# A hybrid encoder block on one core: a fourth early pair of the up-projection, one behind each late token tile

## The chip, the cores and the metric

The kernel runs on one core of a Trainium2 chip. Its time is device time in microseconds of that core; each number below is the median of several executions, or comes from one profiled execution. TensorE multiplies matrices into PSUM (eight banks of 128 x 512 float32), VectorE and ScalarE do elementwise work and read PSUM, GpSimd does small things, and SyncE (SP) and ScalarE issue DMAs. Each engine works its instructions off in order and waits at the head of its queue for what the next one needs.

## What is computed

1024 tokens of width 1024 pass a mixing block (pooling and neighbourhood attention, joined by an output projection with a residual) and a squared-ReLU MLP with a hidden width of 4096, each behind an RMS norm:

```python
def reference(x, norm_mix_g, w_in, w_pool, pool_scale, rpb, w_out,
              norm_mlp_g, w_up, w_down, final_g):
    for l in range(DEPTH):
        h = rmsnorm(x, norm_mix_g[l])
        proj = h @ w_in[l]
        ...
        a = pool_mixer(u, w_pool[l], pool_scale[l])
        b = neighbourhood_attention(q, k, v, rpb[l])
        x = x + jnp.concatenate([a, b], axis=-1) @ w_out[l]
        h = rmsnorm(x, norm_mlp_g[l])
        x = x + jnp.square(jax.nn.relu(h @ w_up[l])) @ w_down[l]
    return rmsnorm(x, final_g)
```

All of it is float32, and DEPTH is 1.

## The kernel before

**Products.** A float32 operand is split into a high part (cast to float32r, on ScalarE) and a low part (what the cast left, on VectorE); each product of two 128-wide blocks is then three matmuls (`three`, lines 143, 145, 147): high by high, high by low, low by high. A *product* in the text below sums four such blocks: 12 matmuls of 128 x 512.

**The MLP's products** are done in Strassen-Winograd form: tokens and the contraction are halved, so that the 1024 x 1024 operand becomes seven operands of 512 x 512 (`ops[1]` to `ops[7]`, tiles `hop`), and `w_up` is taken in 16 *pairs* `b` of 2 x 128 columns, each giving seven products (b, 1) to (b, 7). Products 1 and 2 of a pair need plain parts of the operand (`ops[1]`, `ops[2]`, from the first four token tiles) and plain quarters of the weights; the others need sums. Product 1 goes to a bank `ps_x`, on which products 6 and 7 add later; 2 goes to `ps_e`, 5 and 3 to `ps_w`, 4 to `ps_z`.

**The passage.** After attention the kernel records an order by hand (`manual_schedule`), from one pool of eight PSUM banks (`psum2`, tiles `ps_...`). For each of eight token tiles `tt`:

- `out_tile(tt)`: 24 matmuls of the output projection into two banks (`ps_o`), two VectorE sums with the residual (`acc`), the sum of squares on ScalarE (line 118), `rs` on GpSimd, and `hn`, the normalized tile, on VectorE (line 843, put off into `rest`). SyncE stores the tile to `x2` (line 835) and loads the residual of tile `tt + 2`. Tiles 0 to 3 also prepare the attention's share for tiles 4 to 7: `msp`, a cast and a low part.
- `halfway(tt)`: eight transposes into two banks `ps_t`, then `operands`: copies, casts and low parts of `hop`. Tiles 4 to 7 also form the sums of the Winograd operands.

Between the late tiles stand three *early pairs*: `load_early` (SyncE loads 512 KB, `uraw`), `split_early` (casts and low parts, `us`), `early_pair` (products 1 and 2 of pair `b`, 24 matmuls), and `early_done` (a copy of `ps_x`, a sum with `ps_e`, ReLU and square, and a store of `r11` to DRAM by SyncE, line 870). `EARLY = 3` is their count.

**Low parts** are not recorded at once: `cut2` puts them into a list `lows`; `vec`, which records a VectorE sum, records one low part behind it, and `due(keys)` records all up to those named. What is in the list thus decides which low part VectorE does when.

**The late sequence.** `load_up(b)` loads weights (`wraw`, 1 MB, line 912) into three buffers; `cut(b, i)` forms and splits the weights of a product (`s`); `multiply` records a product; `evacuate` reads it out of its bank: copies (line 999), sums, ReLU and square (lines 855, 856), stores. `seq` is the order of the products: first 2, 3, 4, 5, 6, 7 of the early pairs without 1 and 2, then the seven of pairs 3 to 15. `queue` gives the cuts, five products ahead. `u2` is a pool of 15 buffers for the sums. At the head of this sequence `last_steps` finishes the operands of tile 7. The down-projection follows with the same kind of products (`ps_a`, `ps_b`).

Of the kernel before, what the change touches and what calls it, by code (L numbers as in the profile page):

```python
# [9 lines left out]
F32R = mybir.dt.float32r  # L10
AF = mybir.ActivationFunctionType
ALU = mybir.AluOpType
PSUM = bass.MemoryType.PSUM
# [16 lines left out]
KR = 12  # L30
NPAIR = 16
NARROW, WIDE = 13, 3
EARLY = 3
LOADS, CUTS, STAGGERED = 10, 4, 4


# [1 line left out]
def block_kernel(ctx, tc, x, norm_mix_g, w_in, w_pool, pool_scale, rpb, w_out,  # L38
# [13 lines left out]
    pad0.tile([P, 88], F32, name="padding0")  # L52
    const = ctx.enter_context(tc.tile_pool(name="const", bufs=1))
    dram = ctx.enter_context(tc.tile_pool(name="dram", bufs=1, space=DRAM))
    banks = [tc.tile_pool(name="psum", bufs=2, space=PSUM), tc.tile_pool(name="psum2", bufs=8, space=PSUM)]
    firstp = ExitStack()
    psum = [firstp.enter_context(banks[0])]
    small = ctx.enter_context(tc.tile_pool(name="small", bufs=4))
# [14 lines left out]
    def t4(name, dt=F32):  # L73
        return k4.tile([P, 1024], dt, tag="k4", name=name, bufs=NARROW)
# [632 lines left out]
    ops = {i: t_op(hb) for i in (1, 5, 2, 3, 4)}  # L707
    ops.update({i: t_op(ka) for i in (6, 7)})

    def load_early(b):  # L710
        raw = t4("uraw").rearrange("p (c n) -> p c n", c=NC8)
        nc.sync.dma_start(out=raw, in_=w_up[:, 2 * b * P:(2 * b + 1) * P]
                          .rearrange("(c p) n -> p c n", p=P))
        return raw

    firstp.close()
    psum[0] = ctx.enter_context(banks[1])
# [12 lines left out]
    def due(*keys):  # L730

        while any(k in keys for k, _ in lows):
            lows.pop(0)[1]()
# [6 lines left out]
    def cut2(key, hi, lo, src):  # L740
        nc.scalar.copy(out=hi, in_=src)  # L741
        low(key, lo, src, hi)

    def split_early(raw, b):
        out = []
        for k in range(2):
            s = t4("us", F32R).rearrange("p (l c n) -> p l c n", l=2, c=4)
            cut2(("us", b, k), s[:, 0], s[:, 1], raw[:, 4 * k:4 * k + 4, :])
            out.append(s)
        return out  # L750

    def product(ps, s, t, more=False):

# [19 lines left out]
    def turn(hn):  # L773
        pts = []
        for g in range(2):
            pt = bank("t")
            for k in range(4):
                c = 4 * g + k
                nc.tensor.transpose(pt[:, k * P:(k + 1) * P], hn[:, c * P:(c + 1) * P], ident)
            pts.append(pt.rearrange("p (k t) -> p k t", k=4))  # L780
        return pts
# [38 lines left out]
    nc.sync.dma_start(out=gb2, in_=norm_mlp_g[0].partition_broadcast(P))  # L820
    px, pe, pw, pz = {}, {}, {}, {}
    r11, r12, r21, r22 = {}, {}, {}, {}
    raw_early, early, hns, turned_ = {}, {}, {}, {}
    rest = []

    def out_tile(tt):
        while rest:
            rest.pop(0)()
        a = acc[tt]
        for nh in range(2):  # L830
            nsl = slice(nh * HALF, (nh + 1) * HALF)
            ps = bank("o")
            run(out_half(mb[tt // 4], wos[1], tt, nh, ps))
            vec(a[:, nsl], ps, a[:, nsl], ALU.add)
        nc.sync.dma_start(out=x2[tt * P:(tt + 1) * P, :], in_=a)
        load_acc(tt + 2)
        hns[tt] = t4("hn2")
        rs = rstd([sumsq(a, hns[tt])])
        if tt < 4:
            m = t4("msp", F32R).rearrange("p (l t) -> p l t", l=2)  # L840
            cut2(("mb1", tt), m[:, 0], m[:, 1], bs[tt][:, HALF:])
            mb[1].append(m)
        rest.append(lambda: nc.vector.scalar_tensor_tensor(out=hns[tt], in0=a, scalar=rs, in1=gb2,
                                                           op0=ALU.mult, op1=ALU.mult))

    def halfway(tt):

        steps = operands(turn(hns.pop(tt)), tt)
        steps[:] = steps[:2] + rest + steps[2:]
        rest.clear()  # L850
        for s in steps:
            s()
# [5 lines left out]
    def early_pair(b):  # L858
        due(("us", b, 0), ("us", b, 1), ("op", 1), ("op", 2))
        px[b], pe[b] = bank("x"), bank("e")  # L860
        product(px[b], early[b][0], ops[1])
        product(pe[b], early[b][1], ops[2])

    def early_done(b):
        t = t4("r11")
        r, m = t[:, :HALF], t[:, HALF:]
        nc.scalar.copy(out=m, in_=px[b])
        vec(r, pe[b], m, ALU.add)
        relu_square(r)
        nc.sync.dma_start(out=us[0][b], in_=r)  # L870

    for tt in range(4):
        out_tile(tt)
        if tt:
            halfway(tt - 1)
    raw_early[0] = load_early(0)
    due(*[("mb1", k) for k in range(4)])
    out_tile(4)
    halfway(3)
    raw_early[1] = load_early(1)  # L880
    early[0] = split_early(raw_early[0], 0)
    out_tile(5)
    halfway(4)
    early_pair(0)
    out_tile(6)
    early_done(0)
    raw_early[2] = load_early(2)
    early[1] = split_early(raw_early[1], 1)
    halfway(5)
    out_tile(7)  # L890
    halfway(6)
    early_pair(1)
    while rest:
        rest.pop(0)()
    early[2] = split_early(raw_early[2], 2)
    pts7 = turn(hns.pop(7))
    early_done(1)
    early_pair(2)
    last_steps = operands(pts7, 7)
    last_steps.pop(0)()  # L900
    early_done(2)
    first.close()


# [92 lines left out]
    def copied(ps, name):  # L997
        c = tu(name)
        nc.scalar.copy(out=c, in_=ps)
        return c  # L1000

    def evacuate(b, i):

        if i == 1:
            m1[b] = copied(px[b], "m1")
        elif i == 5:
            m5[b] = copied(pw[b], "m5")
        elif i == 6:
            m16[b] = copied(px[b], "m16")
        elif i == 2:  # L1010
            r11[b] = relu2(pe[b], m1[b])
            stored(1, b, r11[b])
        elif i == 7:
            m167[b] = copied(px[b], "m167")
            r22[b] = relu2(px[b], m5[b])
            stored(4, b, r22[b])
        elif i == 3:
            r12[b] = relu2(pw[b], m16[b])
            if b < EARLY:
                r11[b] = tu("r11")  # L1020
                nc.sync.dma_start(out=r11[b], in_=us[0][b])
        else:
            r21[b] = relu2(m167[b], pz[b], ALU.subtract)
            stored(2, b, r21[b])
            u_sums(b)
# [46 lines left out]
    def cut_pair(i, b):  # L1072
# [11 lines left out]
        if ahead:  # L1084
# [2 lines left out]


    seq = [(0, 5), (0, 6), (1, 5), (1, 6), (0, 7), (0, 3), (0, 4), (2, 5), (2, 6), (1, 7), (1, 3), (1, 4),
           (2, 7), (2, 3), (2, 4)]  # L1090
    seq += [(b, i) for b in range(EARLY, NPAIR) for i in (1, 5, 6, 2, 7, 3, 4)]
    queue = list(seq)
    for k in range(2):
        cut(*queue.pop(0))
        last_steps.pop(0)()
    cut(*queue.pop(0))
    last_steps.pop(0)()
    loads, splits = order_d[:LOADS], order_d[:CUTS]
    for n, x in enumerate(seq):
        while queue and seq.index(queue[0]) <= n + 5:  # L1100
            cut(*queue.pop(0))
        multiply(*x)
        if n >= 1:
            evacuate(*seq[n - 1])
        if lazy and x[1] != 7:
            lazy.pop(0)()
        left = len(seq) - 1 - n
        if left <= 5:
            for _ in range(2):
                if loads:  # L1110
                    load_d(*loads.pop(0))
        if left <= 2:
            cut_pair(*splits.pop(0))
# [154 lines left out]
```

## Time and profile before

| | us |
|---|---|
| median of three runs | 1029.84 (1028.5 to 1030.84) |
| the profiled execution | 1031.89 |
| its span, first to last instruction | 1030.1 |
| TensorE busy | 982.0 (95%) |
| VectorE busy | 662.3 (64%) |
| ScalarE busy | 537.7 (52%) |
| GpSimd busy | 174.8 (17%) |

The mean granted clock of TensorE is 0.981 of full speed. TensorE is nearly always busy, so a share of busy time says little here; what matters is where its 48 us of idle time and the stretches at a lower clock lie. The windows view gives busy time by engine for any stretch, with the granted clock; the timeline gives each instruction with the idle time before it and what ended that; the chain follows the work that ended last.

### The profile page before, as it was taken

To read this page: it belongs to the slowest core of one execution; us is meant where nothing else is said; L and a number is where in the kernel's file an instruction comes from. 1 tells how busy PE (TensorE), PEld (TensorE's weight loads), DVE (VectorE), ACT (ScalarE), POOL (GpSimd) and SP (SyncE) were. 2 spreads that over 40 slices of the span, in tenths; PEclk is the share of its full clock that TensorE was granted. 3 is DMA by queue.
4 is the path that set the end of the run, shared out by engine and by line. 5 is a ranking of instruction groups with operands and counts; after the bars stand their busy time and mean duration, and the time that the engine had idled before them with its cause. 6 is when DMAs were issued, how large, how long until landed. Compare 5 with 4: busy or idle time off the path is not lost.

```text
span 1030.1 us, 13174 instructions
## 1 busy us (share of the span) xinstructions
PE 982.0 (95%) x4508; PEld 811.8 (79%) x4508; DVE 662.3 (64%) x1165; ACT 537.7 (52%) x1045; POOL 174.8 (17%) x228
## 2 busy tenths in 40 slices
PE   7998999999899896599999999999999999999996
PEld 5786888887787774488888888888888888888885
DVE  6512588577665557577656656654677868649774
ACT  6413666567652545366556556555544544445463
POOL 3613436252530110000000000000020202003211
PEclk9999999999899997799999999999999999999998
DMA  8585333504761431465554554528966434355222
GB/s 290 153 236 129 76 94 82 145 23 106 247 209 75 174 132 62 133 214 175 159 171 130 158 168 123 164 82 286 341 221 229 160 104 162 103 203 186 86 102 100
DMA packets 103685, 159.40 MB, mean 155 GB/s; under 512 B 9409, under 2 KB 48833, under 8 KB 103618
## 3 DMA queue, kind: packets, MB, share of 16 engines
q1 hardware_dynamic: 103040, 157.51, 48.2%
q10 hardware_dynamic: 578, 1.05, 0.3%
q8 instruction: 35, 0.57, 0.2%
q14 instruction: 32, 0.26, 0.1%
HBM read 105.83 MB, written 48.27 MB: 150 GB/s over the span
## 4 chain that ended last, share of the span: by engine, by line
PE 83%; DMA 3%; issue 3%; DVE 3%; ACT 2%; POOL 2%; SPq 2%; ACTq 0%; POOLq 0%; DVEq 0%
PE ps_pp L143 5%; PE ps_pp L145 5%; PE ps_pp L147 5%; PE ps_a L145 5%; PE ps_a L143 5%; PE ps_a L147 5%; PE ps_x L147 4%; PE ps_b L145 4%; PE ps_b L143 4%; PE ps_b L147 4%; PE ps_x L143 4%; PE ps_x L145 4%; PE ps_w L143 3%; PE ps_w L145 3%; PE ps_w L147 3%
## 5 line engine op out<-in xcount | busy, mean ns | idle before, releaser
L100 ACT CAST st<-ur 128x512 fp32r<-128x512 f32 x112 | 69.7, 622 | 133.0 <-PE ps_a L147 61.4
L101 DVE TENSOR_TENSOR st<-ur,st 128x512 fp32r<-128x512 f32 x112 | 82.8, 739 | 80.8 <-ACT st L100 80.3
L1130 POOL TENSOR_TENSOR m<-m,x2t 128x512 f32<-128x512 f32 x16 | 27.3, 1729 | 519.0 <-DMA x2t<-x 402.3
L147 PE MATMUL ps_a<-st 128*128 128x512 f32 x256 | 99.7, 390 | 0.0
L143 PE MATMUL ps_a<-st 128*128 128x512 f32 x256 | 99.7, 389 | 0.0
L145 PE MATMUL ps_a<-st 128*128 128x512 f32 x256 | 99.7, 389 | 0.0
L101 DVE TENSOR_TENSOR st<-pq,st 128x512 fp32r<-128x512 f32 x112 | 84.5, 754 | 1.1
L143 PE MATMUL ps_pp<-hh,wh 128*128 128x512 f32 x192 | 76.7, 399 | 2.0 <-DVE q L468 2.0
L145 PE MATMUL ps_pp<-hl,wh 128*128 128x512 f32 x192 | 76.6, 399 | 0.0
L147 PE MATMUL ps_pp<-hh,wl 128*128 128x512 f32 x192 | 76.4, 398 | 0.0
L100 ACT CAST st<-pq 128x512 fp32r<-128x512 f32 x112 | 69.0, 616 | 13.6 <-DVE pq L1077 13.5
L143 PE MATMUL ps_b<-st 128*128 128x512 f32 x192 | 74.8, 390 | 0.0
L145 PE MATMUL ps_b<-st 128*128 128x512 f32 x192 | 74.8, 389 | 0.0
L147 PE MATMUL ps_b<-st 128*128 128x512 f32 x192 | 74.8, 389 | 0.0
L855 ACT ACTIVATE r<-r 128x512 f32<-128x512 f32 x64 | 40.5, 632 | 65.0 <-DVE r L736 65.0
L143 PE MATMUL ps_x<-hop,s 128*128 128x512 f32 x180 | 70.2, 390 | 0.0
L145 PE MATMUL ps_x<-hop,s 128*128 128x512 f32 x180 | 70.1, 390 | 0.0
L147 PE MATMUL ps_x<-hop,s 128*128 128x512 f32 x180 | 70.1, 389 | 0.0
L528 POOL TENSOR_SCALAR s<-s,ri 128x288 f32<-128x288 f32 (+1 forms) x64 | 42.5, 667 | 109.8 <-DVE ri L527 87.3
L143 PE MATMUL ps_w<-hop,s 128*128 128x512 f32 x128 | 50.7, 396 | 10.4 <-ACT s L741 10.4
L728 DVE TENSOR_TENSOR s<-wraw,s 128x512 fp32r<-128x512 f32 x74 | 50.5, 686 | 8.6 <-ACT s L741 8.3
L143 PEld LDWEIGHTS ps_a<-st 128*128 128x128 f32 x256 | 48.1, 188 | 10.0
(216 smaller groups left out, 2438.5 us busy)
## 6 DMA issues: line engine op xcount, KB each, us to landing
ur<-us SPq DMA_DIRECT2D x56, 512.0 KB
us<-r SPq DMA_DIRECT2D x64, 256.0 KB
wraw<-in_w_up_dram SPq DMA_DIRECT2D x16, 1024.0 KB
pq<-in_w_down_dram SPq DMA_DIRECT2D x32, 512.0 KB
us<-s SPq DMA_DIRECT2D x48, 256.0 KB
xt<-in_x_dram SPq DMA_DIRECT2D x15, 512.0 KB
wraw<-in_w_in_dram SPq DMA_DIRECT2D x12, 512.0 KB
woraw<-in_w_out_dram SPq DMA_DIRECT2D x8, 512.0 KB
```

Source lines behind the costliest of these rows:

```text
L100: nc.scalar.copy(out=hi, in_=src)
L101: (lo_eng or nc.vector).tensor_tensor(out=lo, in0=src, in1=r32(hi), op=ALU.subtract)
L143: nc.tensor.matmul(ps, wh, ah, start=first, stop=False, skip_group_check=more)
L145: nc.tensor.matmul(ps, wh, al, start=False, stop=False, skip_group_check=more)
L147: nc.tensor.matmul(ps, wl, ah, start=False, stop=last, skip_group_check=more)
L528: nc.gpsimd.tensor_scalar(out=s[:, :n], in0=s[:, :n], scalar1=ri, scalar2=1.0, op0=ALU.mult, op1=ALU.mult)
L728: lows.append((key, lambda: nc.vector.tensor_tensor(out=lo, in0=src, in1=r32(hi), op=ALU.subtract)))
L855: nc.scalar.activation(out=r, in_=r, func=AF.Relu)
L1130: nc.gpsimd.tensor_tensor(out=c[tt], in0=c[tt], in1=x, op=ALU.add)
```

## The change

`EARLY` becomes 4, and the passage is recorded in another order; nothing of the arithmetic changes.

- **msp.** The casts of the attention's share move into `m_second`: two ahead of tile 0, two behind tiles 0 and 1. Their low parts come earlier with them.
- **Early pairs.** One pair stands behind the transposition of each of tiles 4, 5 and 6, and one behind that of tile 7 (pair 3). The weights of pair `b + 1` are split within `halfway(4 + b)`, behind the finish of pair `b - 1`, and their low parts are recorded before the next tile. `load_early` stands earlier.
- **Finish and stores.** Pairs 0 and 1 are finished in the passage, and ScalarE's queue issues their store. Pairs 2 and 3 stay in their banks until products 4 and 6 of the late sequence; their `r11` stays in a buffer and is not loaded again.
- **Late sequence.** `seq` carries pair 3 as one of the early ones; the first cuts run three products ahead instead of five; reading out a product 1 or 6 is recorded ahead of the following cuts.
- **Banks.** `psum2` is made with `reuse_waits="tile"`, as `ka` and `hb` already are.

```diff
-EARLY = 3
+EARLY = 4
...
-    banks = [tc.tile_pool(name="psum", bufs=2, space=PSUM), tc.tile_pool(name="psum2", bufs=8, space=PSUM)]
+    banks = [tc.tile_pool(name="psum", bufs=2, space=PSUM), tc.tile_pool(name="psum2", bufs=8, space=PSUM, reuse_waits="tile")]
...
-        if tt < 4:
-            m = t4("msp", F32R).rearrange("p (l t) -> p l t", l=2)
-            cut2(("mb1", tt), m[:, 0], m[:, 1], bs[tt][:, HALF:])
-            mb[1].append(m)
...
+    def m_second(h):
+        m = t4("msp", F32R).rearrange("p (l t) -> p l t", l=2)
+        cut2(("mb1", h), m[:, 0], m[:, 1], bs[h][:, HALF:])
+        mb[1].append(m)
...
-        steps[:] = steps[:2] + rest + steps[2:]
+        steps[:] = steps[:2] + rest + ([other] if other else []) + steps[2:]
...
-        nc.sync.dma_start(out=us[0][b], in_=r)
+        nc.scalar.dma_start(out=us[0][b], in_=r)
+
+    m_second(0)
+    m_second(1)
     for tt in range(4):
+        if tt == 3:
+            load_early(0)
         out_tile(tt)
+        if tt < 2:
+            m_second(tt + 2)
         if tt:
             halfway(tt - 1)
-    raw_early[0] = load_early(0)
     due(*[("mb1", k) for k in range(4)])
     out_tile(4)
+    split_early(0)
     halfway(3)
-    raw_early[1] = load_early(1)
-    early[0] = split_early(raw_early[0], 0)
-    out_tile(5)
-    halfway(4)
-    early_pair(0)
-    out_tile(6)
-    early_done(0)
-    raw_early[2] = load_early(2)
-    early[1] = split_early(raw_early[1], 1)
-    halfway(5)
-    out_tile(7)
-    halfway(6)
-    early_pair(1)
+    load_early(1)
+    due(("us", 0, 0), ("us", 0, 1))
+    last = EARLY - 1
+    for b in range(last):
+        out_tile(5 + b)
+
+        def other():
+            if b:
+                early_done(b - 1)
+            split_early(b + 1)
+
+        halfway(4 + b, other)
+        early_pair(b)
+        due(("us", b + 1, 0), ("us", b + 1, 1))
+        if b + 2 < EARLY:
+            load_early(b + 2)
     while rest:
         rest.pop(0)()
-    early[2] = split_early(raw_early[2], 2)
-    pts7 = turn(hns.pop(7))
-    early_done(1)
-    early_pair(2)
-    last_steps = operands(pts7, 7)
-    last_steps.pop(0)()
-    early_done(2)
+    last_steps = operands(turn(hns.pop(7)), 7)
+    early_pair(last)
+    while lows:
+        lows.pop(0)[1]()
...
-            if b < EARLY:
+            if b < EARLY - 2:
                 r11[b] = tu("r11")
                 nc.sync.dma_start(out=r11[b], in_=us[0][b])
...
-           (2, 7), (2, 3), (2, 4)]
+           (3, 5), (3, 6), (2, 7), (2, 3), (2, 4), (3, 7), (3, 3), (3, 4)]
...
-    for k in range(2):
+    for k in range(3):
         cut(*queue.pop(0))
         last_steps.pop(0)()
-    cut(*queue.pop(0))
     last_steps.pop(0)()
...
-        while queue and seq.index(queue[0]) <= n + 5:
+        urgent = n and seq[n - 1][1] in (1, 6)
+        if urgent:
+            evacuate(*seq[n - 1])
+        while queue and seq.index(queue[0]) <= n + (3 if n < 4 else 5):
             cut(*queue.pop(0))
         multiply(*x)
-        if n >= 1:
+        if n in (4, 6):
+            b = last - 3 + n // 2
+            m1[b] = copied(px[b], "m1")
+            evacuate(b, 2)
+        if n and not urgent:
             evacuate(*seq[n - 1])
```

**VectorE around tiles 3 and 4.** Numbers tell buffers apart. Before, from the first sum of tile 3 to the first sum of tile 4 (`acc_3792`); `msp_3859` is the last share that tile 4 needs:

```order
L736 TENSOR_TENSOR acc_3734<-ps_o_3819,acc_3734 128x512
L728 TENSOR_TENSOR hop_3648<-both_3755,hop_3648 128x4x128
L736 TENSOR_TENSOR acc_3734<-ps_o_3834,acc_3734 128x512
L728 TENSOR_TENSOR msp_3801<-bt_2240,msp_3801 128x512
L843 SCALAR_TENSOR_TENSOR hn2_3852<-acc_3734,rs_3857,gb2_3661 128x1024
L728 TENSOR_TENSOR hop_3646<-both_3813,hop_3646 128x4x128
L728 TENSOR_TENSOR hop_3648<-both_3813,hop_3648 128x4x128
L728 TENSOR_TENSOR msp_3859<-bt_2950,msp_3859 128x512
```

Now, from the first sum of tile 0 to the second sum of tile 2:

```order
L738 TENSOR_TENSOR xt_3204<-ps_o_3667,xt_3204 128x512
L730 TENSOR_TENSOR msp_3663<-bt_861,msp_3663 128x512
L738 TENSOR_TENSOR xt_3204<-ps_o_3682,xt_3204 128x512
L730 TENSOR_TENSOR msp_3665<-bt_1523,msp_3665 128x512
L840 SCALAR_TENSOR_TENSOR hn2_3700<-xt_3204,rs_3705,gb2_3661 128x1024
L738 TENSOR_TENSOR acc_3659<-ps_o_3710,acc_3659 128x512
L730 TENSOR_TENSOR msp_3707<-bt_2240,msp_3707 128x512
L738 TENSOR_TENSOR acc_3659<-ps_o_3725,acc_3659 128x512
L840 SCALAR_TENSOR_TENSOR hn2_3742<-acc_3659,rs_3747,gb2_3661 128x1024
L738 TENSOR_TENSOR acc_3698<-ps_o_3767,acc_3698 128x512
L730 TENSOR_TENSOR msp_3749<-bt_2950,msp_3749 128x512
```

All four low parts of `msp` now stand ahead of the second sum of tile 2; the last of them stood behind both sums of tile 3, `hn` and two `hop`.

**SyncE, from the load of the last residual to the late weights.** Before (`us0` is the store of an early pair, `x2` that of a token tile):

```order
L816 DMA acc_3976<-ad_122 128x1024
L835 DMA x2_125<-acc_3913 128x1024
L870 DMA us0_126<-r11_4078 128x512
L712 DMA uraw_4084<-in_w_up_dram 128x8x128
L835 DMA x2_125<-acc_3976 128x1024
L870 DMA us0_126<-r11_4224 128x512
L870 DMA us0_126<-r11_4266 128x512
L912 DMA wraw_4284<-in_w_up_dram 128x8x256
L912 DMA wraw_4286<-in_w_up_dram 128x8x256
L912 DMA wraw_4288<-in_w_up_dram 128x8x256
```

Now, on the same queue from the same load on (`acc`, the residual of tile 7):

```order
L818 DMA acc_3978<-ad_122 128x1024
L714 DMA uraw_4046<-in_w_up_dram 128x8x128
L836 DMA x2_125<-acc_3912 128x1024
L714 DMA uraw_4151<-in_w_up_dram 128x8x128
L836 DMA x2_125<-acc_3978 128x1024
L920 DMA wraw_4308<-in_w_up_dram 128x8x256
L920 DMA wraw_4310<-in_w_up_dram 128x8x256
L920 DMA wraw_4312<-in_w_up_dram 128x8x256
```

No store of an early pair stands on this queue, and the first three `wraw` follow the store of tile 7.

**ScalarE, from the sum of squares of tile 7 to the end of the second pair's finish.** Before:

```order
L118 ACTIVATE hn2_4150,ssq_4151<-acc_3976 128x1024
L801 COPY t_4169<-ps_t_4162 128x512
L741 CAST hop_3647<-t_4167 128x4x128
L741 CAST hop_3651<-t_4168 128x4x128
L741 CAST hop_3652<-both_3871 128x4x128
L741 CAST hop_3650<-both_3871 128x4x128
L741 CAST hop_3649<-t_4169 128x4x128
L741 CAST us_4210<-uraw_4084 128x512
L741 CAST us_4212<-uraw_4084 128x512
L867 COPY r11_4224<-ps_x_4184 128x512
L855 ACTIVATE r11_4224<-r11_4224 128x512
L856 ACTIVATE r11_4224<-r11_4224 128x512
```

Now, on ScalarE between the same two points:

```order
L118 ACTIVATE hn2_4184,ssq_4185<-acc_3978 128x1024
L803 COPY t_4203<-ps_t_4196 128x512
L743 CAST hop_3647<-t_4201 128x4x128
L743 CAST hop_3651<-t_4202 128x4x128
L869 COPY r11_4211<-ps_x_4125 128x512
L857 ACTIVATE r11_4211<-r11_4211 128x512
L858 ACTIVATE r11_4211<-r11_4211 128x512
L872 DMA us0_126<-r11_4211 128x512
L743 CAST us_4218<-uraw_4151 128x512
L743 CAST us_4220<-uraw_4151 128x512
```

The finish of pair 1 with its store (`us0`) now stands ahead of the casts of pair 3's weights (`us_4218`, `us_4220`); before, the casts of the last pair's weights (`us_4210`, `us_4212`) stood ahead of it.

## Rows read from the trace of the kernel before

**Rows 1.** Busy time by engine in two stretches (windows view); columns in the first line.

```profile
core 0: us, PE busy (x) PEld busy (x) DVE busy (x) ACT busy (x) POOL busy (x), PEclk, DMA share, GB/s
328.68:431.13 102.45, 79.44 (x340) 63.55 (x341) 57.92 (x85) 43.32 (x77) 6.66 (x16) 0.87 0.39 130
...
445.00:1008.00 563.00, 563.00 (x2485) 466.50 (x2484) 385.88 (x583) 300.79 (x534) 39.92 (x28) 1.00 0.51 169
```

**Rows 2.** TensorE's timeline; in brackets idle time before the row and its releaser.

```profile
start us, us, engine line op out<-in xcount [idle before <-releaser]
346.84 0.48 PE L143 MATMUL ps_o<-woh,msp 128*128 128x512 f32 x1
...
352.38 1.04 PE L779 MATMUL ps_t<-ident,hn 128*128 128x128 f32 x8
...
353.18 0.47 PE L143 MATMUL ps_o<-woh,msp 128*128 128x512 f32 x1
...
358.60 0.74 PE L147 MATMUL ps_o<-woh,msp 128*128 128x512 f32 x1 [2.64 <-DVE msp L728]
...
372.37 0.50 PE L147 MATMUL ps_x<-hop,us 128*128 128x512 f32 x1 [1.24 <-DVE us L728]
...
391.67 1.09 PE L779 MATMUL ps_t<-ident,hn 128*128 128x128 f32 x8 [2.22 <-DVE hn L843]
...
400.98 1.06 PE L779 MATMUL ps_t<-ident,hn 128*128 128x128 f32 x8 [1.12 <-DVE hn L843]
...
405.15 0.79 PE L143 MATMUL ps_x<-hop,us 128*128 128x512 f32 x1 [3.11 <-ACT us L741]
...
408.68 0.80 PE L147 MATMUL ps_x<-hop,us 128*128 128x512 f32 x1 [2.31 <-DVE us L728]
...
426.48 0.80 PE L143 MATMUL ps_w<-hop,s 128*128 128x512 f32 x1 [10.37 <-ACT s L741]
...
431.13 0.40 PE L143 MATMUL ps_x<-hop,s 128*128 128x512 f32 x1
```

**Rows 3.** SyncE's timeline of DMA issues, same columns.

```profile
368.08 0.43 SPq L712 DMA_DIRECT2D uraw<-in_w_up_dram  x1
...
408.18 10.40 SPq L870 DMA_DIRECT2D us<-r  x2
...
418.67 19.36 SPq L912 DMA_DIRECT2D wraw<-in_w_up_dram  x4
```

**Rows 4.** VectorE's timeline, same columns.

```profile
355.46 1.28 DVE L843 SCALAR_TENSOR_TENSOR hn<-acc,rs,gb 128x1024 f32<-128x1024 f32 x1 [1.58 <-ACT both L791]
...
356.66 1.29 DVE L728 TENSOR_TENSOR hop<-both,hop 128x512 fp32r<-128x512 f32 x2
...
357.86 0.68 DVE L728 TENSOR_TENSOR msp<-bt,msp 128x512 fp32r<-128x512 f32 x1
...
371.63 0.68 DVE L728 TENSOR_TENSOR us<-uraw,us 128x512 fp32r<-128x512 f32 x1
```

**Rows 5.** The chain that ended last, pieces: start us, us, what.

```profile
353.31 1.15 ACT hn L118 x2
...
404.58 1.04 ACT us L741 x2
...
416.95 0.64 ACT r L855
...
418.67 6.39 DMA wraw<-in_w_up_dram
...
425.09 0.70 DVE t L736
...
425.81 0.63 ACT s L741
```

**Rows 6.** ScalarE's timeline near the kernel's end (ACTq is a DMA issue).

```profile
1017.17 0.37 ACTq L1238 DMA_DIRECT2D out_dram<-misc  x1
...
1017.65 0.63 ACT L118 ACTIVATE misc<-m 128x512 f32<-128x512 f32 x1 [0.51 <-DVE m L1228]
```

**Rows 7.** Windows of 1 us, columns as in rows 1.

```profile
374.00:375.00 1.00, 1.00 (x7) 0.81 (x6) 1.00 (x2) 0.00 (x0) 0.00 (x0) 1.00 0.00 0
...
393.00:394.00 1.00, 1.00 (x4) 0.81 (x3) 1.00 (x3) 0.00 (x0) 0.00 (x0) 0.50 0.06 16
```

More of the change, by code (lines that the diff above doesn't have):

```diff
@@ L708, in block_kernel @@
     ops.update({i: t_op(ka) for i in (6, 7)})
+    raw_early, early = {}, {}
     def load_early(b):
@@ L713, in load_early @@
                           .rearrange("(c p) n -> p c n", p=P))
-        return raw
+        raw_early[b] = raw
     firstp.close()
@@ L742, in cut2, with split_early @@
         low(key, lo, src, hi)
-    def split_early(raw, b):
-        out = []
+    def split_early(b):
+        raw, out = raw_early[b], []
         for k in range(2):
@@ L749, in split_early @@
             out.append(s)
-        return out
+        early[b] = out
     def product(ps, s, t, more=False):
@@ L822, in block_kernel @@
     r11, r12, r21, r22 = {}, {}, {}, {}
-    raw_early, early, hns, turned_ = {}, {}, {}, {}
-    rest = []
+    hns, rest = {}, []
     def out_tile(tt):
@@ L838, in out_tile, with halfway @@
         rs = rstd([sumsq(a, hns[tt])])
-        if tt < 4:
-            m = t4("msp", F32R).rearrange("p (l t) -> p l t", l=2)
-            cut2(("mb1", tt), m[:, 0], m[:, 1], bs[tt][:, HALF:])
-            mb[1].append(m)
         rest.append(lambda: nc.vector.scalar_tensor_tensor(out=hns[tt], in0=a, scalar=rs, in1=gb2,
                                                            op0=ALU.mult, op1=ALU.mult))
-    def halfway(tt):
+    def m_second(h):
+        m = t4("msp", F32R).rearrange("p (l t) -> p l t", l=2)
+        cut2(("mb1", h), m[:, 0], m[:, 1], bs[h][:, HALF:])
+        mb[1].append(m)
+    def halfway(tt, other=None):
         steps = operands(turn(hns.pop(tt)), tt)
-        steps[:] = steps[:2] + rest + steps[2:]
+        steps[:] = steps[:2] + rest + ([other] if other else []) + steps[2:]
         rest.clear()
```

## The prediction

> **What bounds the kernel now.** I read the windows first. TensorE works without a break from 445 to 1008 us: 563.00 of 563.00 us at full clock, with VectorE busy for 385.88 and ScalarE for 300.79 of them [rows 1]. Nothing there can be won by moving other engines' work. The hole is the passage from the output projection to the up-projection: from 328.68 (first matmul of `ps_o`) to 431.13 (end of the first late product) TensorE is busy 79.44 of 102.45 us, at a granted clock of 0.87 [rows 1]. The change touches this stretch alone, so the sum is made there.
>
> The TensorE timeline [rows 2] says where the hole is. At full clock 24 matmuls (one token tile of the projection, or one early pair) take 5.54 us, restart included (346.84 to 352.38), and the eight transposes 0.80 (352.38 to 353.18). The stretch holds eight token tiles, three early pairs and half a pair (the first late product), so 11.5 x 5.54, and eight transposes, 6.4: 70.1 us. The loss is 102.45 - 70.1 = **32.3 us**: 23.01 idle, in seven gaps, and about 9.3 of matmuls at the lower clock behind the gaps. The gaps, by what ends them: 2.64 (VectorE's low part of `msp`), 1.24 (low part of `us`), 2.22 and 1.12 (normalized tile `hn`), 3.11 and 2.31 (both parts of `us` for the third pair), 10.37 (first late weights `s`).
>
> The engines behind them: VectorE does `hn` and two `hop` before that `msp` [rows 4]; the weight loads of the late products leave SyncE's queue only at 418.67, behind the store of the last early pair, at whose head the queue had stood since 408.18 [rows 3], and the first takes 6.39 to land [rows 5].
>
> **The change part by part.** I walk the new order from 353.18, up to which nothing that TensorE waits for moves, with these steps: VectorE 0.60 an operation and 1.20 for `hn` [rows 4], ScalarE 0.52 a cast (1.04 for two), VectorE to ScalarE 0.72, ScalarE to another engine 0.67, 2.15 from the start of the sum of squares to `hn` [rows 4, 5], VectorE to TensorE 0.74 [rows 2, 4].
>
> *msp.* Its four low parts now stand behind the first, second, third and fifth sum of the projection, all before tile 3. Tile 4 runs through: 353.18 to 358.72. The 2.64 and the slow matmuls behind it go. What is late next is `hn` of tile 4: sums ready at 358.9, sum of squares 359.6, `hn` from 361.8 to 363.0; its transposes are due at 365.06. Covered.
>
> *Pair 0* is due at 365.86. Its weights, whose load stands one tile earlier on SyncE, are cast before `hop`; the low `hop` starts at 365.4 and is there at 366.14, when the second matmul wants it. No wait, but no slack either.
>
> *A pair after each of tiles 5, 6 and 7.* Each transposition now has a whole pair between its tile and itself, 5.54 us, where tiles 6 and 7 followed each other directly. From the last matmul of a tile to `hn` it takes 0.43 + 0.72 + 2.15 + 1.20, near 4.5 us, plus up to 0.7 when VectorE finishes another operation first: covered by 0.3 to 1.0. So tile 6 runs from 371.40, pair 1 from 377.74, tile 7 from 383.28, pair 2 from 389.62 to 395.16, and the transposes end at 395.96. The gaps of 2.22, 1.12, 3.11 and 2.31 go.
>
> *The fourth pair* adds no TensorE work: its 24 matmuls leave the late list, which falls by two products. They are work for 5.54 us of the former gap.
>
> *What is late next: pair 3.* ScalarE has its weights behind the finish of pair 1. Tile 7's sums are ready at 389.0 (VectorE), then sum of squares 389.75, copies and casts to 392.65, copy of `ps_x`, VectorE's sum after `hn` at 393.81, two activations of 0.64 from 394.5 [rows 5], and then the store that ScalarE now issues itself. That price is in the trace: at the end of the kernel such an issue holds ScalarE from 1017.17 to the next start at 1017.65, 0.48 [rows 6]. So the cast starts at 396.33 and TensorE at 397.0: a new gap of 1.04, and 0.2 for the low part. Pair 3 ends at 402.74.
>
> *Loads.* SyncE no longer holds a store of an early pair, so `wraw` is issued behind the store of tile 7, at 389.9. With 6.39 it lands at 396.3; the tile's store ahead of it is 512 KB where 256 KB were, so I allow 1.2 more, 397.5. VectorE reads it at 401.35, after the last `hop` of tile 6. Hidden, with 4 us to spare. The early weights (512 KB): one issued at 368.08 with another 512 KB beside it left no traffic after 374 [rows 3, 7], so 6 us; wanted at 369.6, 384.4 and 396.3, issued at 363.5, 371.8 and 380.4. Only the first is near.
>
> The Trainium skill ("DMA: Bandwidth & Descriptors", section "Issuing engines are not separate DMA queues") says that DMAs issued from several engines run on the same 16 DMA engines, and that this saves only the issuing time on the sequencer, usually small. By that alone moving two stores would be worth two issues of some 0.3 us, and the sum would be near 17 (the rival of late loads, below). The trace differs: what SyncE lost in [rows 3] was 10 us of standing before a store whose data was not there.
>
> *First late product.* VectorE's queue after pair 3 is full: the raw sum at 401.35, `t` 401.96, ScalarE's cast of `hop` at 403.14, its low part at 403.92. TensorE starts at 403.8 instead of 402.74 (1.06), and its second matmul stands until 404.66 (0.6). It ends at 407.16. Behind it one wait of 0.37 (low part of the fourth product).
>
> *Banks.* Pairs 2 and 3 keep four banks of eight until the late sequence; the first `ps_z` needs that of pair 2, the next `ps_w` that of pair 0. My walk has them free at 420.85 and 423.9, wanted at 421.1 and 423.85: nothing to 0.05. Bank reuse ends no gap in [rows 2], so that its waits become finer is worth nothing here.
>
> *Sum.* Before, 431.13 with three pairs done; after, 407.16 with four: 23.97 + 5.54 = 29.5, less 0.4 for waits behind it: **29.1 us**, or a loss of 3.3 where 32.3 stood. 1031.89 (the profiled execution) less 29.1 is 1002.8; that execution is 2.05 above the median of the three runs, so 1000.7 on the median: **1001 us**. The late sequence has a third of VectorE and half of ScalarE free [rows 1], so I take no loss from its new order.
>
> Bounds of what the trace does not show: the hand-offs at pairs 0 and 3 and the first late product could cost nothing (3.3 better, 997.5) or twice (1004). The new order of the late sequence has no row; its cost lies between 0 and the 3.3 of the entry again, nearest to 0 by [rows 1].
>
> **The rivals.**
>
> *The clock falls once or twice more.* After the gap of 2.22 the clock stood at 0.50, after that of 1.24 at 1.00 [rows 2, 7]. The two new gaps, 1.25 and 1.66, lie between, nearer the lower. A fall to 0.50, the 1.2 GHz level, costs 1.85: transposes and pair behind the gap of 2.22 took from 391.67 to 399.86 (400.98 less 1.12), 8.19 instead of 6.34. One or two: 1002.6 to 1004.4.
>
> *ScalarE and VectorE become the bound of the passage.* Both work without a break from about 389 to 404 in my walk, and each hand-off is in series. If every pair waits 1.5 to 3 us, four pairs and the first products give back 7 to 12 and some clock: 1008 to 1014. For it: slack of 0 to 1 us at pair 0 and at each transposition. Against: tiles 0 to 3 kept that rhythm without a gap.
>
> *The loads stay late after all.* If they wait for the last early pair as before (2.56 from its end, 426.48 less 10.37, to their issue at 418.67, then 6.39), they land near 411.7, 10.3 after VectorE wants them, and the clock falls: 1013. The order on SyncE speaks against it.
>
> *Slower than before.* Eight full banks, and two more `r11` held in the 15 buffers of `u2`. If sums wait for a buffer or bank in every product, TensorE waits through the late sequence: from 0.28 us a product over some 105 products the gain is gone, at 0.4 (42 us) it is 1001 + 42 = 1043. The Trainium skill ("PSUM — Partial Sum Buffer", its summary of rules) asks for prompt evacuation since PSUM is tight, and four banks held over three products go against that. Against it: VectorE is busy 0.69 of the late time [rows 1], 13 us of a pair's 19, so a delay at the entry is worked off and does not repeat.
>
> **How the numbers follow.** Forecast (997.5 to 1002) 0.60; clock 0.20; engines as the bound 0.11; loads late 0.02; slower 0.04; the rest, 0.03, a gain that comes back elsewhere, within 0.2% (2 us, about what a measurement of this kernel tells from no change). The range 997.5 to 1008 takes in the forecast, the clock and a little of the engines' case, some 0.82. Faster 0.93, same 0.03, slower 0.04.
>
> **What would show it.** Right: TensorE's gaps by `msp`, `hn` and `s` gone, transposes 6.3 or 11.9 us apart from 352 on, `wraw` issued near 390 and the first late product near 404; short gaps ended by ScalarE's `us` of pair 3 and by `hop` of the first late product; 1.00 in the late sequence. Wrong: `wraw` as the releaser of VectorE, a clock of 0.50 around 397 or 405, gaps in `ps_z` or `ps_w` ended by VectorE's `r`.

## Result and profile after

The changed kernel takes **1003.3 us** (median of 4 runs, 1001.33 to 1004.8) where the kernel before takes 1030.26 beside it: ratio 0.973 [0.9712, 0.9748]. Forecast was 1001.0, range 997.5 to 1008. Its profiled execution took 1004.8, with a span of 1003.0 where 1030.1 stood.

The windows of the changed kernel, columns as in [rows 1]: first matmul of `ps_o` to the end of the first late product; from there to 462.77; a stretch of 10 us; the rest.

```profile
325.62:404.78 79.16, 77.13 (x366) 62.65 (x365) 58.44 (x87) 42.35 (x76) 6.33 (x16) 1.00 0.53 173
404.78:462.77 57.99, 57.89 (x253) 46.93 (x251) 42.38 (x69) 37.22 (x66) 0.00 (x0) 1.00 0.52 163
462.77:472.36 9.59, 7.20 (x26) 5.75 (x25) 6.92 (x11) 4.94 (x9) 0.00 (x0) 0.82 0.65 198
472.36:994.60 522.24, 522.24 (x2305) 432.25 (x2303) 354.84 (x538) 273.93 (x488) 35.92 (x30) 1.00 0.48 164
```

The first line answers the first of [rows 1]: 79.16 us at full clock with four early pairs where 102.45 at 0.87 stood with three. The third line is new: 2.4 us without a matmul, and a granted clock of 0.82, in a stretch where the kernel before had no break at all.

TensorE's timeline of the changed kernel, against [rows 2]:

```profile
325.26 0.52 PE L548 MATMUL ps_O<-pth,vhl 96*128 96x256 f32 x3
325.62 0.40 PE L143 MATMUL ps_o<-woh,msp 128*128 128x512 f32 x1
...
394.32 0.50 PE L143 MATMUL ps_x<-hop,us 128*128 128x512 f32 x1 [0.72 <-ACT us L743]
...
401.10 0.50 PE L143 MATMUL ps_w<-hop,s 128*128 128x512 f32 x1 [0.76 <-ACT hop L743]
402.15 0.50 PE L145 MATMUL ps_w<-hop,s 128*128 128x512 f32 x1 [0.55 <-DVE hop L730]
...
404.78 0.39 PE L143 MATMUL ps_x<-hop,s 128*128 128x512 f32 x1
...
465.17 0.50 PE L143 MATMUL ps_x<-hop,s 128*128 128x512 f32 x1 [2.40 <-ACT m L1007]
...
467.00 0.63 PE L143 MATMUL ps_x<-hop,s 128*128 128x512 f32 x1
...
994.37 0.39 PE L147 MATMUL ps_a<-st 128*128 128x512 f32 x1
```

All seven gaps of [rows 2] are gone. Three short ones stand in the passage, all three forecast, and a fourth at 465 that was not: the second product of pair 4 adds onto `ps_x` and has to wait until ScalarE has copied `m1` out of it.

To compare traces I cut each at three matmuls: the last `ps_O` (325.26 here), the first of the second late product (404.78) and the last of all (994.37). **A** is the first piece, the passage, **B** the second. For kernels with three early pairs, 5.45 us (24 matmuls of 0.227) are moved from B to A, so that all do the same work. Before: A 326.69 to 431.13, 104.44 + 5.45 = **109.89**; B 431.13 to 1021.42, 590.29 - 5.45 = **584.84**. After: A **79.52**, B **589.59**. So the passage gave 30.37, the late sequence took back 4.75, and 1.43 more is what both executions differ by ahead of the passage (326.69 against 325.26), where the programs are alike: 27.05 in all. Over the 14 traces of this study the last `ps_O` lies anywhere between 323.16 and 327.62, so that last part is no work of the change.

Behind the gap at 465 stands a chain that the trace shows row by row. SyncE, VectorE and ScalarE in the changed kernel:

```profile
438.90 0.38 SPq L920 DMA_DIRECT2D wraw<-in_w_up_dram  x1
439.34 0.83 SPq L1029 DMA_DIRECT2D r<-us  x1
```

```profile
431.95 0.69 DVE L738 TENSOR_TENSOR s<-s,r 128x512 f32<-128x512 f32 x1 [2.21 <-DMA r<-us]
...
447.80 0.69 DVE L738 TENSOR_TENSOR s<-s,r 128x512 f32<-128x512 f32 x1 [4.54 <-issue]
```

```profile
450.33 0.63 ACT L857 ACTIVATE r<-r 128x512 f32<-128x512 f32 x1 [3.92 <-DVE r L738]
...
464.01 0.63 ACT L858 ACTIVATE r<-r 128x512 f32<-128x512 f32 x1
464.55 0.57 ACT L1007 COPY m<-ps_x 128x512 f32<-128x512 f32 x1
```

The sums of pairs 0 and 1 need their `r11` back from memory. The second reload is issued at 439.34 behind a 1 MB load. VectorE stands for it until 447.80. The profile sees no releaser ("issue"), but the DMA row of 438 to 448 us, in 40 slices of 0.25 us, falls from its full rate at 447.0 to nothing at 447.75:

```profile
DMA  0199999888996999969778999999999999997410
```

VectorE's wait becomes ScalarE's (3.92). From there ScalarE's row is nearly full, and the copy of `m1` comes 2.40 late. That this chain is the cause, and not only a row of waits, is what the first two experiments test.

### The profile page after: what moved, and what is told of

It is laid out like the page before. It is cut to its first block, busy times and chain, and to the rows that moved or that the text cites. A ratio compares the mean times of both kernels' runs of the same rounds, so it can differ in the third digit from the quotient of the medians.

```text
span 1003.0 us, 13171 instructions
## 1 busy us (share of the span) xinstructions
PE 976.5 (97%) x4508; PEld 807.2 (80%) x4508; DVE 661.6 (66%) x1165; ACT 537.8 (54%) x1045; POOL 168.9 (17%) x228
## 4 chain that ended last, share of the span: by engine, by line
PE 81%; DVE 5%; ACT 4%; issue 4%; DMA 3%; POOL 2%; SPq 0%; ACTq 0%; POOLq 0%; DVEq 0%
PE ps_pp L143 6%; PE ps_pp L145 6%; PE ps_pp L147 6%; PE ps_a L143 5%; PE ps_a L145 5%; PE ps_a L147 5%; PE ps_b L143 4%; PE ps_b L147 4%; PE ps_b L145 4%; PE ps_x L147 3%; PE ps_x L145 3%; PE ps_x L143 3%; PE ps_O L548 2%; PE ps_w L145 2%; PE ps_w L147 2%
## 5 line engine op out<-in xcount | busy, mean ns | idle before, releaser
L101 DVE TENSOR_TENSOR st<-pq,st 128x512 fp32r<-128x512 f32 x112 | 82.3, 735 | 1.1
L143 PE MATMUL ps_x<-hop,s 128*128 128x512 f32 x176 | 69.1, 392 | 2.4 <-ACT m L1007 2.4
L147 PE MATMUL ps_x<-hop,s 128*128 128x512 f32 x176 | 69.3, 394 | 0.1
L145 PE MATMUL ps_x<-hop,s 128*128 128x512 f32 x176 | 69.1, 393 | 0.0
L147 PEld LDWEIGHTS ps_a<-st 128*128 128x128 f32 x256 | 48.0, 188 | 10.1
L143 PEld LDWEIGHTS ps_a<-st 128*128 128x128 f32 x256 | 48.0, 188 | 9.9
```

What stands on the lines that cost most here:

```text
L101: (lo_eng or nc.vector).tensor_tensor(out=lo, in0=src, in1=r32(hi), op=ALU.subtract)
L143: nc.tensor.matmul(ps, wh, ah, start=first, stop=False, skip_group_check=more)
L145: nc.tensor.matmul(ps, wh, al, start=False, stop=False, skip_group_check=more)
L147: nc.tensor.matmul(ps, wl, ah, start=False, stop=last, skip_group_check=more)
```

## Experiments

**Early reloads.**

```diff
+    for b in range(EARLY - 2):
+        r11[b] = tu("r11")
+        nc.sync.dma_start(out=r11[b], in_=us[0][b])
     def stored(i, b, src):
...
-            if b < EARLY - 2:
-                r11[b] = tu("r11")
-                nc.sync.dma_start(out=r11[b], in_=us[0][b])
```

> The changed kernel, but the two reloads of `r11` (pairs 0 and 1) are issued right behind the first three loads of `wraw` instead of behind the pair's third product. Reload theory (VectorE stands 2.21 and 4.54 us before the sums with the reloaded tile, ScalarE then runs late, and its copy of pair 4's `m1` holds TensorE at 465 for 2.40 us and some 2.2 of lower clock): both waits of VectorE go, the gap at 465 goes, and the time falls by 3 to 5 us, to about 999. Rival, the order on ScalarE (the copy of `m1` stands behind ten activations of pairs 0 to 3 whatever the reloads do): VectorE's waits go, but a gap of 1 us or more before the second product of pair 4 stays, and the time falls by under 2 us.

1000.01 us, ratio 0.9707 [0.9677, 0.9737]. A 79.52, as in the changed kernel; B 585.24, 4.35 less, and 1.84 less than in the changed kernel's other execution (587.08, below). The medians are 3.3 apart, with intervals that touch, so the traces carry this. Both waits of VectorE are gone. SyncE's row, and the windows from the first `ps_o` to pair 4's second product (460.76 here), and from there to the end:

```profile
395.81 2.74 SPq L960 DMA_DIRECT2D r<-us  x2
```

```profile
323.81:402.97 79.16, 77.14 (x366) 62.67 (x365) 58.45 (x87) 42.36 (x76) 6.32 (x16) 1.00 0.55 180
402.97:460.76 57.79, 57.74 (x253) 47.13 (x252) 45.73 (x74) 40.84 (x71) 0.00 (x0) 1.00 0.52 168
460.76:988.44 527.68, 527.68 (x2329) 436.82 (x2327) 357.62 (x544) 275.61 (x491) 36.00 (x30) 1.00 0.49 165
```

From 460.76 on TensorE doesn't stop. The reload theory holds: with the waits of VectorE gone, the same order on ScalarE costs nothing.

**Copies in their old place.**

```diff
-        urgent = n and seq[n - 1][1] in (1, 6)
-        if urgent:
-            evacuate(*seq[n - 1])
...
-        if n and not urgent:
+        if n:
             evacuate(*seq[n - 1])
```

> The changed kernel, but the copies after a pair's first and third product stand behind the next product's cuts again, as in the kernel before, instead of ahead of them. Order theory (this new place on ScalarE made the gap at 465): the gap goes and the time falls by 3 to 5 us. Reload theory: the copy of `m1` comes one or two casts later, 0.5 to 1.1 us, so the gap at 465 grows to 3 or 3.5 and the time rises by 0.5 to 1.5 us; a product (b, 6) behind a (b, 5) may wait as well.

1002.86 us, 0.9734 [0.9705, 0.9763]: not told apart from the changed kernel. B is 586.60. VectorE's wait and TensorE's gap in this execution:

```profile
447.39 0.69 DVE L738 TENSOR_TENSOR s<-s,r 128x512 f32<-128x512 f32 x1 [2.83 <-issue]
```

```profile
465.28 0.50 PE L143 MATMUL ps_x<-hop,s 128*128 128x512 f32 x1 [1.29 <-ACT m L1007]
```

The gap stays, so the new place of the copies did not make it. But it is smaller, which neither theory had, and so is the wait, which varies between executions. Over six traces the gap follows the sum of VectorE's two reload waits:

| kernel | wait for the first reload | wait for the second | gap at pair 4's second product | both waits less the gap |
|---|---|---|---|---|
| changed | 2.21 | 4.54 | 2.40 | 4.35 |
| changed, once more | 1.98 | 3.90 | 1.51 | 4.37 |
| `msp` late | 2.00 | 3.78 | 1.42 | 4.36 |
| stores on SyncE | 2.00 | 3.73 | 1.37 | 4.36 |
| coarse banks | 1.89 | 3.68 | 1.25 | 4.32 |
| copies in their old place | 1.88 | 2.83 | 1.29 | 3.42 |

With the new place the late sequence covers some 4.35 us of the two waits together, and TensorE stands for what goes beyond it. With the old place it covers 3.42 in the one trace that there is: the old place takes 0.9 of it, near the 0.5 to 1.1 that the reload theory had for the later copy. So the new place helps, and is not the cause. One reload wait alone, 2.41 with three pairs (below), is covered.

**Stores back on SyncE.**

```diff
-        nc.scalar.dma_start(out=us[0][b], in_=r)
+        nc.sync.dma_start(out=us[0][b], in_=r)
```

> The changed kernel, but the two early stores go back to SyncE's queue. The prediction's account (a store whose data is not there holds SyncE and the loads behind it): the first `wraw` leaves only when pair 1's `r` is there, near 395 instead of 387.55, and lands near 401 to 403 instead of 395; VectorE wants it at 399, so the first late product starts 2 to 4 us later; ScalarE saves 0.48 before the cast of pair 3. In all 1 to 5 us slower, more if the clock falls. Rival (moving an issue between queues is worth only the issue itself): within 1 us of the changed kernel.

1005.81 us, 0.9761 [0.9726, 0.9796]; the interval reaches that of the changed kernel, so the trace decides: A 82.36, 2.84 more. SyncE and TensorE:

```profile
393.46 0.32 SPq L872 DMA_DIRECT2D us<-r  x1
393.88 20.77 SPq L920 DMA_DIRECT2D wraw<-in_w_up_dram  x4
```

```profile
394.00 0.50 PE L143 MATMUL ps_x<-hop,us 128*128 128x512 f32 x1 [0.21 <-ACT us L743]
402.68 0.50 PE L143 MATMUL ps_w<-hop,s 128*128 128x512 f32 x1 [2.68 <-ACT hop L743]
```

VectorE, at its first read of `wraw`:

```profile
400.27 0.69 DVE L738 TENSOR_TENSOR t<-wraw 128x512 f32<-128x512 f32 x1 [1.82 <-DMA wraw<-in_w_up_dram]
```

`wraw` leaves at 393.88, behind the store whose data was late, instead of 387.55. VectorE then stands 1.82 for it, where it took it without a wait in the changed kernel, and the first late product waits 2.68 instead of 0.76. Pair 3 gains 0.51 (0.21 for 0.72), since ScalarE issues nothing ahead of its casts. The gaps alone make 1.92 - 0.51 = 1.41; the other 1.43 of the 2.84 go with a lower clock behind the longer gap, which the changed kernel doesn't have there:

```profile
402.00:410.00 8.00, 6.78 (x21) 5.19 (x22) 7.80 (x14) 4.41 (x9) 0.00 (x0) 0.79 0.43 135
```

The Trainium skill ("DMA: Bandwidth & Descriptors", section "Issuing engines are not separate DMA queues") says that issuing from several engines saves only the issue's own time. Here the trace differs: the issue cost ScalarE 0.5, and what was won is the standing of the queue behind it.

**`msp` alone**, in the kernel before (`m_second` as in the change), and **`msp` late**, in the changed kernel.

```diff
+    m_second(0)
+    m_second(1)
     for tt in range(4):
         out_tile(tt)
+        if tt < 2:
+            m_second(tt + 2)
```

> The kernel before with one part of the change: the four `msp` of the second half are cast and cut one to three tiles earlier. The prediction's account: the gap of 2.64 at 358.60 and the slow matmuls behind it (about 1.9) go, and with them 2.6 to 4.5 us of the time: 1026 to 1027.5 where the kernel before takes 1030. Rival (the passage is bound by VectorE's queue, so that what is gained at tile 4 is waited for at `hn` and `us`): the gaps behind it grow by as much, and the time stays within 1 us.

1027.45 us, 0.9971 [0.9953, 0.9989]. A 106.74, 3.15 less. The gap of 2.64 is gone, but two of the gaps behind it have grown, by 0.97 (with 0.28 ahead of it) and 1.61, and one by `us` has shrunk by 0.57 (2.54 for 3.11):

```profile
369.97 0.79 PE L147 MATMUL ps_x<-hop,us 128*128 128x512 f32 x1 [1.93 <-DVE us L728]
...
399.98 1.64 PE L779 MATMUL ps_t<-ident,hn 128*128 128x128 f32 x8 [2.73 <-DVE hn L839]
```

So the rival holds for the idle time, of which the gaps of the passage lose only 0.58 in sum. The other 2.57 of the 3.15 are matmuls that no longer run at the lower clock (TensorE is busy 76.87 where it was 79.44).

```diff
-    m_second(0)
-    m_second(1)
     for tt in range(4):
...
-        if tt < 2:
-            m_second(tt + 2)
+        m_second(tt)
```

> The changed kernel with the four `msp` of the second half made where the kernel before makes them, behind each tile. The prediction's account: the gap ahead of tile 4 is back, 2 to 3 us ended by VectorE's low part of `msp`, with 1.9 of lower clock behind it: 3 to 5 us slower, 1006 to 1008. Rival (in the new order the low parts ahead of sums drain in time, and the earlier cast is worth nothing any more): within 1 us of the changed kernel.

1006.0 us, 0.9767 [0.9748, 0.9787]. A 83.94, 4.42 more, with the old gap back to the hundredth and some 1.7 of slower matmuls behind it:

```profile
357.99 0.50 PE L147 MATMUL ps_o<-woh,msp 128*128 128x512 f32 x1 [2.64 <-DVE msp L730]
```

So the step is worth 4.42 in the new order, where nothing behind it takes the gain, and 3.15 alone.

**Three pairs.**

```diff
-EARLY = 4
+EARLY = 3
...
+    out_tile(7)
+    halfway(6, lambda: early_done(1))
     while rest:
         rest.pop(0)()
```

> The changed kernel with three early pairs: pairs 0 and 1 behind tiles 5 and 6, the transpositions of tiles 6 and 7 one behind the other after tile 7, then pair 2. All else (early `msp`, stores on ScalarE's queue, low parts ahead of sums) stays. The prediction's account (a transposition needs a pair between its tile and itself, and the fourth pair fills 5.54 us of a hole): TensorE waits some 3.7 us (4.5 from the tile's last matmul to `hn`, less 0.80 of the transposition between) for `hn` of tile 7, with or without 1.85 of lower clock behind it, and pair 2 or the first late product 0 to 2 us more; in all 3 to 7 us slower than the changed kernel, 1006 to 1010. Rival (the order and the queues carry the whole gain, and the fourth pair only moves work that the late sequence does as well): within 1.5 us of it.

The edit also takes pair 3's products 3 to 7 out of the head of `seq`. 1007.2 us, 0.9789 [0.9751, 0.9827]. A 82.47 + 5.45 = 87.92, 8.40 more than with four: 4.5 of longer gaps, the rest of matmuls at the lower clock. The two gaps:

```profile
389.23 1.97 PE L781 MATMUL ps_t<-ident,hn 128*128 128x128 f32 x8 [4.14 <-DVE hn L840]
...
400.37 0.50 PE L143 MATMUL ps_w<-hop,s 128*128 128x512 f32 x1 [1.85 <-ACT hop L743]
```

The second of them is no matter of transpositions: VectorE stands 2.54 for a DMA ahead of its first read of `wraw`. By the traces the whole is only 3.4 slower than the changed kernel (3.9 by the medians, which come from two jobs), because B is 584.58: here only the first reload is waited for (2.41), and nothing stops at pair 4. The fourth pair gave 8.4 in the passage, and the late order that comes with it took 5.0 back in that execution of the changed kernel.

**Coarse banks**, in the changed kernel, and **fine banks**, in the kernel before.

```diff
-tc.tile_pool(name="psum2", bufs=8, space=PSUM, reuse_waits="tile")
+tc.tile_pool(name="psum2", bufs=8, space=PSUM)
```

> The changed kernel without the finer reuse of PSUM banks. The prediction's account (no bank's reuse ends a gap): within 1 us, no gap of TensorE more than before. Rival (four banks held over three products make the next bank's wait matter, and with coarse waits a product stands until all earlier users of the pool are done): gaps before `ps_w`, `ps_z` or `ps_x` of 0.5 us or more between 400 and 440, 1 to 5 us slower.

1004.2 us, 0.9741 [0.9718, 0.9764]. None of the rival's gaps, but one that both missed, ahead of the first `ps_o`:

```profile
326.85 0.47 PE L143 MATMUL ps_o<-woh,msp 128*128 128x512 f32 x1 [1.47 <-DVE bt L563]
```

The kernel before has it too (its first `ps_o` starts 1.99 behind the last `ps_O`); in the changed kernel the distance is 0.36. A is 80.70, so the finer reuse is worth 1.18. The reverse edit in the kernel before:

> The kernel before with one part of the change: the finer reuse of the second PSUM pool. The prediction says that this is worth nothing. The run with coarse banks speaks against it: there, as before, TensorE stands 1.47 us for `bt` (VectorE, line 563) ahead of the first `ps_o`, and in the changed kernel it doesn't. If that wait belongs to the coarse banks, it goes here, the first `ps_o` starts some 0.36 us after the last `ps_O` instead of 1.99, and the kernel is 1.6 us faster, unless the gap at `msp` grows by as much. If it is chance, it stands here too, and the time is within 1 us.

1029.88 us, 0.9992 [0.9975, 1.001]. The gap is gone here too:

```profile
323.26 0.52 PE L548 MATMUL ps_O<-pth,vhl 96*128 96x256 f32 x3
323.62 0.40 PE L143 MATMUL ps_o<-woh,msp 128*128 128x512 f32 x1
```

In all 14 traces of this study it stands with coarse banks (3) and not with fine ones (11). But A is 109.38, only 0.51 less than before: the gap at `msp` is the same 2.64, and a wait for `hn` further on is 1.61 longer (2.73 for 1.12), one for `us` 0.87 shorter (2.24 for 3.11).

**What is left of the passage.** Early reloads, with the weights' casts ahead of the finish of the pair before; and beside that tile 7's operands ahead of the first late cut.

```diff
         def other():
+            split_early(b + 1)
             if b:
                 early_done(b - 1)
-            split_early(b + 1)
...
     for k in range(3):
-        cut(*queue.pop(0))
         last_steps.pop(0)()
+        cut(*queue.pop(0))
```

> The run with early reloads (1000.0 us), and ScalarE casts the next pair's weights ahead of the finish of the pair before. The prediction's account (pair 3's gap of 0.7 comes from ScalarE's row of copy, two activations and an issue before the casts): that gap goes, 0.5 to 0.7 us faster, about 999.4. Rival: the copies that free `ps_x` and `ps_e` come 1.1 us later and VectorE's row shifts, so that the first late product waits 0.7 longer and nothing is won.

> As the run before it, and the operands of tile 7 are made ahead of the first cut of late weights instead of behind it. If the order of these two on VectorE sets the gaps of 0.76 and 0.55 at the first late product, `hop` is there 0.6 us earlier and the two gaps fall to 0.7 in sum, unless `s` of the first late product is then the last: 0 to 0.6 us faster. Rival: the second low part or the second product waits instead, and the sum of the gaps stays at 1.3.

999.99 us, 0.9699 [0.9677, 0.9721], and 998.97, 0.9695 [0.9669, 0.9721]. A is 78.78 and 78.46, B 585.32 and 585.42: 0.74 and 0.32 from the two edits, where 0.5 to 0.7 and 0 to 0.6 were expected. In the second run `s` of the first late product has become the last (gaps of 0.38 and 0.60 where 0.83 and 0.56 stood). The medians can't show either step.

**The changed kernel and the last one above ("combined") once more, in one job**, five rounds.

> The changed kernel once more, as the measure for the run beside it: 1003.3, with the gap at 465 of 1 to 2.5 us again, in size as the wait of VectorE for the second reload of `r11`.

> The changed kernel with early reloads of `r11`, the weights' casts ahead of the finish of the pair before, and tile 7's operands ahead of the first late cut, beside the changed kernel in the same job. By the gaps in their traces it saves 2.40 and 1.75 at 465, 0.5 at pair 3 and 0.3 at the first late product: 4 to 5 us faster, near 998.7. If the gap at 465 is rare outside profiled executions, the difference is under 2 us.

The changed kernel 1001.02, 0.9725 [0.9706, 0.9744]; the combined one 999.84, 0.9706 [0.9692, 0.9721]. A 79.52 and 78.45, B 587.08 and 585.43: 2.7 by the traces, 1.2 by the medians, and the intervals touch. The changed kernel's gap at 465 was 1.51 in this execution, and the clock stayed at 1.00 behind it, so its loss was 2.2 and not 4.75. The 4 to 5 us that were expected did not come, and the changed kernel's median was 2.3 below that of the first job. Under 2 us was expected if the gap is rare outside profiled executions, and that stays open. By its traces the combined version is the best of the study; the medians of the one job that holds both put it 1.2 us ahead, which their intervals do not settle.

## Why the prediction was right, and where it was not

Its passage is right in mechanism and nearly in size. Two terms that it put at nothing, the banks and the late sequence, are wrong, with opposite signs.

- *The walk.* It starts at the transposes of 352.38, which stand at 349.77 after, 2.61 earlier. With 2.61 taken off, pair 3 was due at 394.39 and came at 394.32, `wraw` at 387.29 and 387.55, the first late product at 401.19 and 401.10, its end at 404.55 and 404.78. In all A gave 30.37, of which the banks make 1.18; the other 29.19 stand against the 29.5 of the sum.
- *msp*: the 2.64 and the slow matmuls behind it were to go; undoing the step costs 4.42 (the gap and some 1.7 of clock).
- *A pair after each tile, and the fourth pair*: the gaps of [rows 2] by `hn` and `us` went. Without the fourth the wait for `hn` was 4.14, where the walk's steps had given 3.7.
- *The store on ScalarE*: 0.48 forecast; pair 3's gap shrank by 0.51 without it. That it spares SyncE's queue was right too: 1.92 of gap and 1.43 of clock. This is for the stores of pairs 0 and 1. The largest gap before, 10.37, stood behind the store of the last pair, which the new order takes out of the passage altogether. That `wraw` now leaves at 387.55 and 0.76 is left of the gap is read from rows; no run undoes that part.
- *The new gaps*: 1.04, 1.06 and 0.6 forecast, 0.72, 0.76 and 0.55 measured. *The clock* stayed at 1.00 through the passage, so the rival that it falls there failed, as did the rivals of late loads and of the engines as the bound. In the profiled execution it fell at 465 instead, for 1.75.
- *Banks*: **wrong.** "Bank reuse ends no gap in [rows 2], so that its waits become finer is worth nothing here": my window began at the first `ps_o`, just behind the gap of 1.47 that it does end, and I had not asked what held that first matmul. Four banks held over three products cost some 0.3 us, where the walk had 0 to 0.05 at the `ps_w` that needs the bank of pair 0. Its first matmul comes 0.40 after the one before and the next 0.34, where 0.23 stands elsewhere, and it starts 0.75 behind VectorE's start on that bank, the walk's step from VectorE to TensorE (0.74); five other traces have the same distance (0.74 or 0.75). No other stall by a bank of the early pairs is in the changed kernel's rows. The Trainium skill ("PSUM — Partial Sum Buffer", its summary of rules) asks for prompt evacuation; the trace shows this small price for going against it. TensorE and VectorE there:

```profile
421.68 0.50 PE L143 MATMUL ps_w<-hop,s 128*128 128x512 f32 x1
```

```profile
420.93 0.69 DVE L738 TENSOR_TENSOR r<-ps_x,m 128x512 f32<-128x512 f32 x1 [1.17 <-ACT m L1007]
```

- *The late sequence*: **wrong**, and the step that failed. "The late sequence has a third of VectorE and half of ScalarE free, so I take no loss from its new order": it lost 4.75 in the profiled execution, above the bound of 3.3, and 2.24 in another. With the reloads early 0.40 of it is left, which is what the prediction allowed for waits there. A mean of busy shares doesn't tell whether one late transfer falls into a dense stretch. The wait was there to be read in the kernel before, hidden:

```profile
453.65 0.69 DVE L736 TENSOR_TENSOR s<-s,r 128x512 f32<-128x512 f32 x1 [2.47 <-DMA r<-us]
```

There it was 2.47 for the first reload alone, and no gap of TensorE follows. In the new order the second reload is wanted early as well: VectorE is ready for it at 443.26, 3.9 after its issue, and stands 2.83 to 4.54 in six traces; with the 1.88 to 2.21 for the first this is more than the late sequence covers. The rival "slower than before" had waits of the sums in it, but for buffers and banks, and repeated in every product; it is two waits, for two loads, and nothing repeats.

The profiled execution came out 2.0 above the 1002.8 of the sum: 4.35 more late loss than allowed and 0.3 less from the walk, against it the banks' 1.18 and the 1.43 ahead of the passage. So part of its nearness is luck: the banks' gain was not foreseen, and the 1.43 is no work of the change. The median was 2.3 above the forecast in the first job and on it in the second (1001.02), a difference that no run explains.

Open: undone one at a time, `msp`, the fourth pair, the two stores and the banks cost 4.42, 8.40, 2.84 and 1.18, 16.8 of the 30.37, and single steps need not add up. The rest (early weights loaded and cast sooner, their low parts ahead of the next tile, the late finish of the last pairs) was not undone by itself; that it closed the gaps by `us` and `s` is argued from the rows.

Why the second reload's wait varies from 2.83 to 4.54 between executions was not tried apart. The DMA row shows full rate until it lands, the load of 1 MB ahead of it among that; whether that load or the late issue makes the wait is not shown.

## What to carry to other kernels

Cost a queue by what stands at its head. Moving a store to another queue costs that queue one issue (0.5 here) and frees the loads that stood behind its late data (6.3 us earlier here). Where work is pulled forward, look for reloads that are then wanted sooner, and issue them well ahead of their use: here at 395.81, behind the first three bulk loads, instead of at 426.56 and 439.34. And begin the window of a sum one instruction ahead of the gap that seems to be the first.

## What was not expected of the hardware

The granted clock after a gap. Behind the gap of 2.40 matmuls took 0.63 from the sixth on (467.00 is the seventh) and then 0.39 again, at a cost of 1.75 us for one product (4.39 instead of 2.72, and 0.08 after it; some 0.1 of this is the restart, since behind a gap without a fall the same product took 2.85 to 2.87); behind the single gaps of 1.25 to 1.51 us in the five other traces of the table it stayed at 1.00. Behind 2.64 (`msp`) and 2.68 (stores on SyncE) it fell as well, and also behind 1.85 where 0.55 followed one matmul later (three pairs: 0.54 from 403.4 to 405.4). The windows of 464 to 472 us, changed kernel and the same kernel in its other execution:

```profile
464.00:472.00 8.00, 6.83 (x23) 5.47 (x24) 5.43 (x10) 3.73 (x7) 0.00 (x0) 0.79 0.64 186
```

```profile
464.00:472.00 8.00, 7.06 (x31) 5.87 (x32) 6.84 (x11) 4.80 (x9) 0.00 (x0) 1.00 0.74 195
```

So 0.89 us of gap more (2.40 for 1.51) went with 2.51 more of B, and two executions of one kernel differ by that.
